# A 192-byte and a 128-byte padding that move where the tiles of a three-layer fp32 kernel begin in SBUF

## Chip, cores and metric

The kernel runs on one core of one Trainium2 chip. The time is the device time of one execution in microseconds; of several executions the median counts. Profiles are of one execution, taken by the hardware profiler. SBUF is the on-chip memory of 128 partitions from which all engines read; a tile's address is a byte offset that is the same in each partition.

## What is computed

Two blocks act on a sequence of 512 tokens with 1,024 features, all in fp32. The first has two layers, the second one. Cut to what costs time:

```python
# first block, layer 0: gated 3-tap convolution beside 8-head attention with low-rank q, k, v and rope
x = x + rms_norm(parallel_conv_mla(rms_norm(x, g0), ...), g1)
x = x + rms_norm(square(relu(rms_norm(x, g2) @ w1)) @ w2, g3)      # w1 1024x4096, w2 4096x1024
# layer 1: 31-tap depthwise convolution between two pointwise products, layer norm, silu
x = x + rms_norm(conformer_conv(rms_norm(x, g4), ...), g5)
x = x + rms_norm(square(relu(rms_norm(x, g6) @ w1)) @ w2, g7)
# second block, one layer: 16 meta tokens in front, forgetting attention (8 heads), pooling, swiglu
h = h + concat(attention, pooled) @ w_out
h = h + (silu(n2 @ w_gate) * (n2 @ w_up)) @ w_down                 # 1024x2816 twice, 2816x1024
```

Nearly all of it is matrix products of weights with all 512 tokens.

## The kernel before, in words

Activations lie with features on partitions and tokens along the row. Every fp32 operand of a product is split into two fp32r parts, a rounded one (plane 0, "hi") and the rest (plane 1, "lo"), and every product is made of three TensorE matmuls (`mm3`, lines 357 to 359): hi weights by hi tokens, hi weights by lo tokens, lo weights by hi tokens. A matmul has a stationary operand of 128 columns, loaded first by LDWEIGHTS (the profile's PEld), and a moving operand of up to 512 columns that streams past it.

The tiles come from pools, and where a pool's tiles lie follows from the order in which the pools and the constants are laid out, with nothing that chooses an address:

- pool `c`, the constants: `vec` (all small vectors in one table), `eps`, `ones`, `onesf`, `ident`, `bd` and others, made in `consts` and `late_consts`
- pool `p`, 32 token tiles named `P` of 4,096 bytes in each partition: the split activations (two planes of 512), pairs of unsplit ones, and the split q, k, v and probabilities of both attentions
- pool `s`, nine scratch tiles `S` of 2,176 bytes
- pool `r`, three raw weight tiles `raw` of 4,096 bytes; SP's queue loads 512 KB into one at a time (line 271)
- pool `w`, nine split weight tiles `W` of 4,096 bytes: up to four 128-column pieces, hi plane at the start, lo plane 2,048 bytes on. ScalarE rounds (line 284) and VectorE, or GpSimd in the convolution's stage, subtracts (line 286), four tiles ahead of TensorE

In most matmuls the moving operand is a `P` tile and the stationary one a slice of a `W` tile; the profile writes such a group `ps<-P,W`. In the products that make v with tokens as rows it is the other way round (`ps<-W,P`). In attention's scores (line 623) and in its products with v (again lines 357 to 359) both are `P` tiles, and the profile writes `ps<-P`. The `P` tiles' slices begin at multiples of 256 bytes within the tile in nearly all of these; exceptions are the taps of the convolution (`run_pe`), whose moving operand begins at one of 16 successive 4-byte elements, and masked scores that begin at 96, 224 or 352 elements.

The order of the work is the order in which the program is written (two hand-written orders, `B1` and `B2`, interleave attention with other products); no planner chooses it. In the convolution's stage four of eight channel groups run on TensorE (`run_pe`, 384 matmuls of 256 columns) and four on VectorE (line 1082), some taps at a time between TensorE's products (`tick`); the layer norm behind it (line 1177 on) needs both.

Of the kernel before, what the change touches and what calls it, by code (L numbers as in the profile page):

```python
# [11 lines left out]
F32 = mybir.dt.float32  # L12
# [7 lines left out]
DRAM = bass.MemoryType.DRAM  # L20
# [283 lines left out]
class Program:  # L304
# [171 lines left out]

    def consts(self):
        nc, cp = self.nc, self.cpool
        self.vec = cp.tile([128, self.nv], F32, name="vec")
        nc.sync.dma_start(out=self.vec, in_=self.ap["vec"])  # L480
        self.eps = cp.tile([128, 1], F32, name="eps")
        nc.vector.memset(self.eps, EPS)
        self.halfpi = cp.tile([128, 1], F32, name="halfpi")
        nc.vector.memset(self.halfpi, math.pi / 2)
        self.ones = cp.tile([128, 128], F32R, name="ones")
        nc.vector.memset(self.ones.bitcast(F32), 1.0)
        self.onesf = cp.tile([128, 128], F32, name="onesf")
        nc.vector.memset(self.onesf, 1.0)
# [1230 lines left out]
def build(arrays, stop=None):  # L1719
    nc = bacc.Bacc("TRN2", target_bir_lowering=False, num_devices=1)  # L1720
    ap = {}
    for name, a in arrays.items():
        ap[name] = nc.dram_tensor(f"in_{name}", a.shape, mybir.dt.from_np(a.dtype), kind="ExternalInput").ap()
    ap["out"] = nc.dram_tensor("out_0", (D, T), F32, kind="ExternalOutput").ap()
    with tile.TileContext(nc) as tc:
        with tc.tile_pool(name="c", bufs=1) as cp, tc.tile_pool(name="p", bufs=NP) as pp, \
                tc.tile_pool(name="s", bufs=NS) as sp, tc.tile_pool(name="ps", bufs=8, space=PSUM) as psp, \
                tc.tile_pool(name="d", bufs=1, space=DRAM) as dp, \
                tc.tile_pool(name="r", bufs=3) as rp, tc.tile_pool(name="w", bufs=NW) as wp:
            Program(tc, ap, (cp, pp, sp, psp, dp, rp, wp), stop).run()  # L1730
    return nc

# [6 lines left out]
```

## Time and profile before

| | |
|---|---|
| median of 3 runs | 1793.89 us (1792.48 to 1795.05) |
| the profiled execution's own time | 1788.58 us |
| its span, first to last instruction | 1786.8 us |
| TensorE busy | 1746.1 us, 98% of the span |
| VectorE, ScalarE, GpSimd busy | 61%, 45%, 15% |
| mean granted TensorE clock | 0.996 of full speed |

An engine's busy time is the union of its instructions' durations. A matmul's duration overlaps the next one's, so it says little about the pace; the distance from one matmul's start to the next one's start does.

### The profile page before, as it was taken

Reading aid. Unit: us, or ns where it says so; the run is one execution under the profiler, and the core shown is the slowest. Engines: PE = TensorE matmul, PEld = TensorE weight load, DVE = VectorE, ACT = ScalarE, POOL = GpSimd, SP = SyncE. Lnnn points to the kernel's source line nnn. Section 1 sums busy time; section 2 is a strip of 40 time slices with the busy share of each in tenths; the row PEclk is TensorE's granted clock in tenths of the full one; section 3 lists DMA queues with packets and bytes.
Section 4 is the critical chain, followed back from the end, with each engine's and each line's share of the span. In section 5 each row is a group of like instructions: output and inputs, shape, how many; then the busy total and the mean of one; then the engine's idle time right before and its main releaser. Section 6 shows DMA issues by size and latency. Waiting matters only on the chain.

```text
span 1786.8 us, 23140 instructions
## 1 busy us (share of the span) xinstructions
PE 1746.1 (98%) x8828; PEld 1455.2 (81%) x8828; DVE 1092.6 (61%) x1770; ACT 802.0 (45%) x1461; POOL 272.4 (15%) x339
## 2 busy tenths in 40 slices
PE   9999999999999999999999999989999999999999
PEld 7778888888888878998888888888787888888887
DVE  7988685344444789968544444488896554344442
ACT  6546655333333446576433333357675443232230
POOL 3413330000000365503000000042223200000000
PEclk9999999999999999999999999999999999999999
DMA  5232213222222133512222222222222222222221
GB/s 200 68 101 59 101 60 118 94 95 94 95 94 95 48 106 106 166 59 91 100 95 94 95 95 95 94 95 73 72 73 95 94 95 94 95 94 95 94 95 59
DMA packets 49887, 167.26 MB, mean 94 GB/s; under 512 B 6848, under 2 KB 7296, under 8 KB 49776
## 3 DMA queue, kind: packets, MB, share of 16 engines
q1 hardware_dynamic: 47776, 160.70, 27.0%
q0 software_dynamic: 1936, 5.07, 1.0%
q8 instruction: 69, 1.13, 0.3%
q14 instruction: 42, 0.34, 0.1%
q10 hardware_dynamic: 64, 0.02, 0.0%
HBM read 158.25 MB, written 4.19 MB: 91 GB/s over the span
## 4 chain that ended last, share of the span: by engine, by line
PE 81%; DVE 11%; issue 3%; ACT 2%; POOL 2%; DMA 1%; SPq 0%; POOLq 0%; DVEq 0%; ACTq 0%
PE ps L358 26%; PE ps L357 26%; PE ps L359 26%; DVE P L968 2%; DVE W L286 1%; PE ps L623 1%; DVE P L401 1%; DVE S L424 1%; POOL P L971 1%; ACT S L450 1%; DVE S L1477 1%; DVE P L398 1%; DVE S L422 1%; DMA P<-in_xT 1%; DVE P L636 0%
## 5 line engine op out<-in xcount | busy, mean ns | idle before, releaser
L357 PE MATMUL ps<-P,W 128*128 128x512 f32 (+1 forms) x2541 | 935.2, 368 | 6.9 <-DVE S L1130 3.1
L358 PE MATMUL ps<-P,W 128*128 128x512 f32 (+1 forms) x2541 | 932.1, 367 | 5.8 <-DVE P L401 5.8
L359 PE MATMUL ps<-P,W 128*128 128x512 f32 (+1 forms) x2541 | 930.9, 367 | 0.0
L284 ACT ACTIVATE W<-raw 128x512 fp32r<-128x512 f32 x578 | 356.9, 628 | 672.9 <-PE ps L359 586.3
L286 DVE TENSOR_TENSOR W<-raw,W 128x512 fp32r<-128x512 f32 x523 | 372.2, 719 | 396.8 <-ACT W L284 391.1
L357 PEld LDWEIGHTS ps<-P,W 128*128 128x128 f32 x2541 | 479.9, 189 | 93.2 <-DVE S L1130 3.5
L358 PEld LDWEIGHTS ps<-P,W 128*128 128x128 f32 x2541 | 480.3, 189 | 90.2 <-DVE P L401 7.2
L359 PEld LDWEIGHTS ps<-P,W 128*128 128x128 f32 x2541 | 480.0, 189 | 84.4 <-DVE W L286 0.4
L971 POOL TENSOR_TENSOR P<-P 128x256 f32<-128x256 f32 x48 | 45.5, 957 | 787.9 <-DVE P L968 786.8
L398 DVE TENSOR_TENSOR P<-S,P 128x512 fp32r<-128x512 f32 (+3 forms) x134 | 93.8, 705 | 50.5 <-ACT P L397 49.9
L397 ACT ACTIVATE P<-S 128x512 fp32r<-128x512 f32 (+3 forms) x134 | 81.4, 613 | 63.2 <-DVE S L1664 25.8
L286 POOL TENSOR_TENSOR W<-raw,W 128x512 fp32r<-128x512 f32 x55 | 73.6, 1369 | 38.0 <-ACT W L284 33.9
L1082 DVE SCALAR_TENSOR_TENSOR ps<-P,vec,ps 128x512 f32<-128x512 f32 x116 | 77.8, 745 | 0.0
L1029 DVE SCALAR_TENSOR_TENSOR S<-ps,S 128x512 f32<-128x512 f32 x64 | 43.7, 690 | 37.0 <-PE ps L359 36.7
L400 ACT ACTIVATE P<-P,vec 128x256 fp32r<-128x256 f32 (+1 forms) x80 | 43.7, 550 | 49.8 <-POOL P L971 30.3
L470 POOL TENSOR_TENSOR S<-S 128x256 f32<-128x256 f32 (+1 forms) x45 | 47.6, 1058 | 76.0 <-ACT S L469 73.6
L401 DVE SCALAR_TENSOR_TENSOR P<-P,vec 128x256 fp32r<-128x256 f32 (+1 forms) x80 | 53.2, 678 | 9.7 <-ACT P L400 9.5
L469 ACT ACTIVATE S<-P 128x256 f32<-128x256 f32 (+1 forms) x105 | 46.4, 473 | 17.8 <-DVE P L1056 11.8
L636 POOL TENSOR_TENSOR P<-S,P 128x512 fp32r<-128x512 f32 (+1 forms) x24 | 34.3, 1428 | 113.0 <-DVE P L635 96.1
L1049 DVE TENSOR_TENSOR P<-ps,P 128x512 f32<-128x512 f32 x42 | 29.1, 692 | 30.9 <-PE ps L359 30.9
L623 PE MATMUL ps<-P 128*128 128x512 f32 (+3 forms) x160 | 41.3, 376 | 1.8 <-DVE S L1443 0.8
L470 DVE TENSOR_TENSOR S<-S 128x256 f32<-128x256 f32 (+1 forms) x60 | 33.0, 550 | 14.5 <-ACT S L469 13.5
(262 smaller groups left out, 1295.6 us busy)
## 6 DMA issues: line engine op xcount, KB each, us to landing
raw<-in_w SPq DMA_DIRECT2D x286, 512.0 KB
P<-in_xT SPq DMA_DIRECT2D x8, 256.0 KB
P<-in_xT POOLq DMA_DIRECT2D x8, 256.0 KB, 5.6
keep<-P SPq DMA_DIRECT2D x8, 256.0 KB
P<-P SPq DMA_DIRECT2D x16, 128.0 KB
P<-keep POOLq DMA_DIRECT2D x8, 256.0 KB, 4.6
out<-P SPq DMA_DIRECT2D x7, 256.0 KB
raw<-in_w SPq DMA_DIRECT2D x2, 256.0 KB
```

The costliest lines, as they stand in the source:

```text
L284: nc.scalar.activation(out=w[:, 0, :cols], in_=r, func=AF.Copy)
L286: eng.tensor_sub(out=w[:, 1, :cols], in0=r, in1=w[:, 0, :cols].bitcast(F32))
L357: mm(ps, w[0], x[0], start=first, stop=False)
L358: mm(ps, w[0], x[1], start=False, stop=False)
L359: mm(ps, w[1], x[0], start=False, stop=last)
L397: nc.scalar.activation(out=hi, in_=src, func=AF.Copy)
L398: nc.vector.tensor_sub(out=lo, in0=src, in1=hi.bitcast(F32))
L401: nc.vector.scalar_tensor_tensor(out=lo, in0=src, scalar=scale, in1=hi.bitcast(F32), op0=OP.mult, op1=OP.subtract)
L470: (eng or nc.vector).tensor_add(out=acc, in0=acc, in1=t)
L623: mm(o[:m], k, q[:, pl, c0:], start=n == 0 and m == 128, stop=n == len(keys) - 1 and mask is None)
L971: ins = eng.tensor_add(out=x[k][:, cols], in0=x[k][:, cols], in1=m[k][:, cols]).ins
L1082: V.scalar_tensor_tensor(out=dst if dst is not None and t == taps[-1] else acc, in0=u, scalar=w, in1=acc, op0=OP.mult, op1=OP.add)
```

## The change

`consts` takes one more tile of 48 floats (192 bytes) in front of `vec`, and a new pool with one tile of 32 floats (128 bytes) stands in front of the pools of raw and split weights. Each is written once, in one column, by a memset on VectorE.

```
     def consts(self):
         nc, cp = self.nc, self.cpool
+        g0 = cp.tile([128, 48], F32, name="pad0")
+        nc.vector.memset(g0[:, 0:1], 0.0)
         self.vec = cp.tile([128, self.nv], F32, name="vec")
...
-                tc.tile_pool(name="d", bufs=1, space=DRAM) as dp, \
+                tc.tile_pool(name="d", bufs=1, space=DRAM) as dp, tc.tile_pool(name="pad", bufs=1) as pad, \
                 tc.tile_pool(name="r", bufs=3) as rp, tc.tile_pool(name="w", bufs=NW) as wp:
+
+            nc.vector.memset(pad.tile([128, 32], F32, name="pad")[:, 0:1], 0.0)
             Program(tc, ap, (cp, pp, sp, psp, dp, rp, wp), stop).run()
```

The built programs place the tiles so (bytes in each partition; the remainder is of the division by 256, the same for all tiles of a pool but `S`):

| tiles | first address before | remainder | first address after | remainder |
|---|---|---|---|---|
| `ones`, `onesf`, `ident`, `bd` | 18240 | 64 | 18432 | 0 |
| `P` | 28736 | 64 | 28928 | 0 |
| `S` | 159808 | 64 and 192 | 160000 | 0 and 128 |
| `raw` | 179392 | 192 | 179712 | 0 |
| `W` | 191680 | 192 | 192000 | 0 |

On all engines the two programs are the same, instruction by instruction, but for the two memsets at the start of VectorE's stream. The piece of the difference on VectorE, at the program's start (`pad` is the new pool's tile, `pad_80` the one in front of the constants; line numbers grow by the added lines):

```order
-L1725 UNCONDITIONAL_BRANCH
-L482 MEMSET eps 128x1
-L484 MEMSET halfpi 128x1
-L486 MEMSET ones 128x128
-L488 MEMSET onesf 128x128
+L1727 UNCONDITIONAL_BRANCH
+L1733 MEMSET pad 128x1
+L480 MEMSET pad_80 128x1
+L484 MEMSET eps 128x1
+L486 MEMSET halfpi 128x1
+L488 MEMSET ones 128x128
+L490 MEMSET onesf 128x128
```

The four memsets that were there move back by two places; nothing else moves.

## Rows read from the trace of the kernel before

**Rows 1.** The page: span, and busy time of each engine.

```profile
span 1786.8 us, 23140 instructions
...
PE 1746.1 (98%) x8828; PEld 1455.2 (81%) x8828; DVE 1092.6 (61%) x1770; ACT 802.0 (45%) x1461; POOL 272.4 (15%) x339
```

**Rows 2.** Matmul groups of line 357, forms kept apart (tiles, shape, count, busy, mean, idle).

```profile
L357 PE MATMUL ps<-P,W 128*128 128x512 f32 x1879 | 743.4, 396 | 5.0 <-DVE S L1130 3.1 <-ACT P L400 1.0 <-ACT W L284 0.9
...
L357 PE MATMUL ps<-P,W 128*128 128x256 f32 x654 | 188.6, 289 | 1.9 <-ACT P L397 0.8 <-ACT P L400 0.6 <-DVE P L1689 0.5
...
L357 PE MATMUL ps<-W,P 128*128 128x256 f32 x80 | 22.9, 286 | 0.0
```

**Rows 3.** Timeline of TensorE in the first MLP (start, duration, instruction).

```profile
449.67 0.40 PE L357 MATMUL ps<-P,W 128*128 128x512 f32 x1
...
455.94 0.40 PE L357 MATMUL ps<-P,W 128*128 128x512 f32 x1
```

**Rows 4.** Timeline of TensorE at the end of the first attention.

```profile
185.53 4.28 PE L623 MATMUL ps<-P 128*128 128x512 f32 x18
189.65 0.39 PE L359 MATMUL ps<-P 128*128 128x512 f32 x1
...
190.56 0.39 PE L357 MATMUL ps<-P 128*128 128x512 f32 x1
...
198.72 0.40 PE L357 MATMUL ps<-P,W 128*128 128x512 f32 x1
```

**Rows 5.** Busy time of engines in two stretches, with clock, DMA share, GB/s.

```profile
190.56:198.72 8.16, 8.16 (x37) 6.76 (x36) 7.21 (x9) 5.40 (x11) 3.28 (x2) 1.00 0.01 3
449.67:455.94 6.27, 6.27 (x29) 5.08 (x27) 3.29 (x5) 2.55 (x5) 0.00 (x0) 1.00 0.33 120
```

**Rows 6.** Timeline of TensorE in products over half the tokens.

```profile
255.48 0.28 PE L357 MATMUL ps<-P,W 128*128 128x256 f32 x1
...
257.97 0.28 PE L357 MATMUL ps<-P,W 128*128 128x256 f32 x1
```

**Rows 7.** Timeline of TensorE in the second attention's maxima.

```profile
1263.23 0.26 PE L1474 MATMUL ps<-P 128*128 128x32 f32 x1
1263.35 0.19 PE L1475 MATMUL ps<-negq,identb 128*128 128x32 bf16 x1
```

**Rows 8.** Matmul groups of line 357 between 645 and 750 us.

```profile
L357 PE MATMUL ps<-P,W 128*128 128x256 f32 x128 | 36.0, 282 | 0.0
...
L357 PE MATMUL ps<-P,W 128*128 128x512 f32 x80 | 31.7, 396 | 3.1 <-DVE S L1130 3.1
```

**Rows 9.** Busy PE, PEld, DVE, ACT, POOL: attention, convolution, second attention.

```profile
62.00:240.00 178.00, 176.25 (x860) 145.71 (x861) 143.83 (x227) 100.69 (x183) 55.37 (x74) 1.00 0.25 81
645.00:750.00 105.00, 102.63 (x628) 91.62 (x629) 104.87 (x159) 54.53 (x93) 60.62 (x61) 1.00 0.38 123
1210.00:1370.00 160.00, 150.63 (x1014) 122.35 (x1014) 137.60 (x276) 106.95 (x225) 37.91 (x45) 0.99 0.23 69
```

**Rows 10.** Timeline of VectorE at the convolution's last taps.

```profile
747.26 1.40 DVE L1082 SCALAR_TENSOR_TENSOR P<-P,vec,ps 128x512 f32<-128x512 f32 x2
```

**Rows 11.** Timeline of TensorE at the layer norm's first sums.

```profile
749.28 2.97 PE L1177 MATMUL ps<-P,onesf 128*128 128x256 f32 x13
```

**Rows 12.** Timeline of the first microseconds, all engines.

```profile
0.89 0.06 DVE L482 MEMSET eps<- 128x1 f32 x1 [0.89 <-PEq L1720]
...
1.20 4.13 PE L722 MATMUL ps<-ones 128*128 128x512 f32 x11 [1.20 <-DVE ones L486]
...
6.25 0.50 PE L357 MATMUL ps<-P,W 128*128 128x512 f32 x1 [0.92 <-ACT W L284]
```

**Rows 13.** The chain that ended last, a piece near the start.

```profile
2.19 4.80 DMA P<-in_xT
```

**Rows 14.** Timeline of TensorE in the first attention, right after `W` products.

```profile
161.93 0.40 PE L357 MATMUL ps<-P 128*128 128x512 f32 x1
...
162.63 0.39 PE L357 MATMUL ps<-P 128*128 128x512 f32 x1
```

## The prediction

> **What bounds the kernel now.** The page comes first: TensorE is busy for 1746.1 of 1786.8 us, the next engine, VectorE, for 61% [rows 1]. So whatever changes TensorE's pace changes the time, and what it waits for is little. The groups by form say what it does with its time: line 357 makes 1,879 matmuls of 512 columns with a `W` tile as weights, and lines 358 and 359 as many, 5,637 in all; 654 times three of 256 columns with `W` as weights, and 80 times three with `W` as the moving operand, 2,202 in all [rows 2]. Their mean durations overlap and give no pace, so I go to the timeline and divide the distance of two starts by the number of matmuls between them.
>
> In the first MLP, 27 steps take 455.94 - 449.67 = 6.27 us, 232.2 ns each [rows 3]. At the end of the first attention the same lines and line 623 run with a `P` tile as weights and a `P` tile as moving operand, with the same 512 columns: 36 steps take 198.72 - 190.56 = 8.16 us, 226.7 ns each [rows 4]. (The stretch counts 37 matmuls with the one already running; the first stretch 29, with the one running and the one that just begins [rows 5].) The clock isn't the reason: both stretches have 1.00 of the full 2.4 GHz. Nor is the other engines' traffic: in the quicker stretch VectorE is busy for 7.21 of 8.16 us, in the slower for 3.29 of 6.27; transfers run in the slower one (0.33 against 0.01), but the same stages keep their pace between loads. What differs is which tiles meet. In all of the slower ones one operand begins 64 bytes past a multiple of 256 and the other 192; in the quicker ones both begin at 64. And `P` tiles lie all over the first 160 KB, so it is not that the two are near each other.
>
> **The change part by part.** (a) *The two memsets.* VectorE's small memset takes 0.06 us [rows 12], so `ones` and the warm-up matmuls that wait for it start up to 0.12 us later. The warm-up ends at 1.20 + 4.13 = 5.33, and the first real matmul starts at 6.25 because it waits for ScalarE's first `W`, which waits for weights [rows 12]: 0.92 us of cover, price nothing; without it 0.12 us.
>
> (b) *The engines' other operands.* `raw` and `W` move together, and so do `P`, `S` and the constants. ScalarE, VectorE and GpSimd never read one of each kind in an instruction, so no pair of theirs changes its relation; only TensorE reads across. Price nothing.
>
> (c) *TensorE, 512 columns.* `P` and `W` now both begin at remainder 0. I take it that what counts is the distance of the two operands modulo 256 bytes: 128 before, 0 after, as for the quicker pairs. Bounds: 0, if it is something else about `W` tiles, and 232.2 - 226.7 = 5.5 ns for each of 5,637 matmuls, 31.0 us. I take the upper end, since the same lines of code make both paces and only the tiles differ.
>
> (d) *TensorE, 256 columns.* 21 steps take 257.97 - 255.48 = 2.49 us, 118.6 ns each [rows 6]. Half of 226.7 would be 113.3, a gain of 5.3. But a matmul of 32 columns with 128 columns of weights holds the next one off for 0.12 us, 0.11 to 0.13 by the rounded starts [rows 7], so the weight load may itself be the floor here and the gain nothing. Between 0 and 5.3 I take 4, nearer to the upper end, since the rows at 512 columns have the same kind of load and are 5.5 apart. Of the 2,202, 3 x 128 = 384 are taps [rows 8], whose moving operand begins at another 4-byte element every three matmuls: distance 0 only now and then, gain 0 (at most 5.3 ns each, 2.0 us). The other 1,818 give 7.3 us, between 0 and 9.6.
>
> (e) *Settling.* Behind `W` products the quick pace comes only after some nine matmuls: the first 18 of that stretch take 189.65 - 185.53 = 4.12 us, 0.04 more than at 226.7 [rows 4]. With some 40 fresh starts, behind waits and behind other kinds of matmul, that is 1.5 us.
>
> (f) *Where TensorE can't use it.* In the convolution VectorE is busy for 104.87 of 105 us [rows 9], its last tap ends at 747.26 + 1.40 = 748.66 [rows 10], and TensorE comes to the sums that need it at 749.28 [rows 11]. So a quicker TensorE will wait there: the 3 x 80 matmuls of 512 columns [rows 8] at 5.5 ns, 1.3 us, are lost. In the two attentions VectorE is busy for 143.83 of 178 and 137.60 of 160 us [rows 9], and chains of VectorE and ScalarE end some of TensorE's waits; these 338 us are 19% of the span, of (c) and (d) 7.2 us, and I give back half, 3.6. Of the first 62 us, where transfers and VectorE lead, half of 1.3.
>
> Sum: 31.0 + 7.3 - 1.5 - 1.3 - 3.6 - 0.6 = 31.3 us. The profiled execution would go from 1788.6 (its span from 1786.8) to 1757; it was 5.3 us under the median of 1793.9, and I take the same difference from that: **1762.5 us**, 1.7% faster. With every loss at nothing and the upper bounds it is 31.0 + 9.6 + 2.0 = 42.6 us; two timeline stamps rounded to 10 ns add 0.4 ns a step, 2 us: 1749.
>
> **A rule that speaks against it.** The Trainium skill, "TensorE: Matmul & The Clock Gate", section "Step-by-step: what each phase is for", says that TensorE reads SBUF through two independent ports, one for the moving operand and one for the weights, and that loading the next weights takes no bandwidth from the running matmul. By that, where the two lie to each other would not matter, and (c) and (d) would be 0. The trace has 226.7 against 232.2 ns for the same work, which that rule does not explain.
>
> **The rivals.** *Nothing changes.* What slows `W` matmuls is something that the paddings leave as it is: their place far up in SBUF (all nine lie above 191 KB, where no quick pair is seen), or that they are written while others are read. Then only the transfers differ: the first token tiles take 4.80 us to land [rows 13], and 6% of two such, 0.6 us, is the most that I see to gain: 1793.3 to 1793.9. For it: no row shows a `W` tile at the quick pace. Against it: TensorE's pace in `W` stretches is the same while VectorE is idle or busy, and `P` tiles between 28 and 160 KB all mix freely. The skill's "DMA: Bandwidth & Descriptors", section "How a descriptor splits into AXI transactions", names blocks of 256 bytes at whose boundaries a transfer is cut, so 4,096 bytes at remainder 192 would touch 17 instead of 16; an estimate by it is that 6%. No row here shows an aligned one.
>
> *Slower: the same remainder collides.* If two streams at the same remainder meet in the same part of SBUF, and the quick pace is a state that only long undisturbed stretches reach, `W` matmuls may stay in what precedes it: 162.63 - 161.93 = 0.70 us for three, 233.3 ns [rows 14], 1.1 ns above 232.2, 6 us over 5,637; with 235, as the rounding allows, 16 us: 1800 to 1810. It decides as soon as the mean stays above 232.2. Against it: the one long stretch settles after nine and stays so.
>
> *Half of it.* Only part of the matmuls settles, because each `W` slice is used for only two or three of them, or the waits in attention take more back than half: 8 to 20 us, 1774 to 1786.
>
> **How the numbers follow.** All or most of the gain 0.72 (1745 to 1774), half of it 0.08, nothing 0.14, slower 0.06. Within 0.2% of 1793.9, some 3.6 us, is about what a measurement tells from no change; the gain and half of it lie below that, so faster 0.80, same 0.14, slower 0.06. The range 1745 to 1788 takes in the first two and leaves out 0.20.
>
> **What would show it.** Right: in the first MLP starts 226 to 227 ns apart, not 230 to 241; 256-column products of lines 357 to 359 at 113 to 116; a wait of TensorE of 1 to 3 us in front of line 1177; VectorE's and ScalarE's durations as before. Wrong: `W` stretches still at 232.2 (then it is the tiles' place or kind), or a quicker pace in the MLPs with new waits of more than 10 us in all elsewhere.

## The result, and the profile after

The changed kernel takes 1761.67 us (median of 4 runs, 1758.98 to 1763.81) against 1794.07 us (4 runs, 1792.48 to 1795.05) in the same comparison: ratio 0.9819, 95% interval 0.9802 to 0.9836, so 1.8% less time, 32.4 us. The forecast was 1762.5 us. The profiled execution took 1762.84 us. Ratios are of executions in the usual state: one of the kernel with the front padding alone, 1906.75 us at a granted clock of 0.847, is left out of its ratio.

The profile of the kernel after has the same instructions and two memsets more; what has shrunk is TensorE's busy time, by 22 us [rows 1]. The operands' work on ScalarE and VectorE has the durations of before (ScalarE's rounding 628 ns both times):

```profile
span 1761.1 us, 23142 instructions
...
PE 1724.0 (98%) x8828; PEld 1460.4 (83%) x8828; DVE 1091.2 (62%) x1772; ACT 801.6 (46%) x1461; POOL 274.0 (16%) x339
...
L284 ACT ACTIVATE W<-raw 128x512 fp32r<-128x512 f32 x578 | 356.6, 628 | 649.9 <-PE ps L359 608.5
L286 DVE TENSOR_TENSOR W<-raw,W 128x512 fp32r<-128x512 f32 x523 | 371.0, 717 | 378.7 <-ACT W L284 376.1
```

The matmul groups of line 357, forms kept apart, answer to [rows 2]. The matmul of 512 columns lasts 392 ns on average instead of 396, which again says little, since durations overlap; that of 256 columns lasts 290 instead of 289:

```profile
L357 PE MATMUL ps<-P,W 128*128 128x512 f32 x1879 | 736.2, 392 | 3.6 <-DVE S L1132 2.8 <-ACT W L284 0.7
...
L357 PE MATMUL ps<-P,W 128*128 128x256 f32 x654 | 189.4, 290 | 1.3 <-ACT P L397 0.8 <-DVE P L1691 0.5
```

The starts say what happened. TensorE's timeline after, first in the products over half the tokens (it answers to [rows 6]; columns are start, duration, instruction), then in the first MLP (to [rows 3]):

```profile
253.33 0.28 PE L357 MATMUL ps<-P,W 128*128 128x256 f32 x1
...
255.84 0.28 PE L357 MATMUL ps<-P,W 128*128 128x256 f32 x1
...
443.12 0.39 PE L357 MATMUL ps<-P,W 128*128 128x512 f32 x1
...
449.24 0.39 PE L357 MATMUL ps<-P,W 128*128 128x512 f32 x1
```

From 443.12 to 449.24 there are 27 steps again: 6.12 us, 226.7 ns each, where it was 232.2. From 253.33 to 255.84 there are 21: 2.51 us, 119.5 ns each, where it was 118.6. So the quick pace has come to these products of 512 columns and not to these of 256; over the whole trace 96% of the 512-column steps with `W` are at 228 ns or less, where it was 8%.

Windows of the kernel after (busy PE, PEld, DVE, ACT, POOL, granted clock, DMA share, GB/s), in order: the first attention, the first MLP, the convolution from its first 512-column product to the layer norm's first sum, the second MLP, the second attention:

```profile
62.00:238.00 176.00, 175.08 (x866) 146.00 (x865) 143.69 (x226) 100.35 (x183) 55.33 (x74) 1.00 0.26 81
276.00:590.30 314.30, 314.30 (x1447) 262.81 (x1446) 142.07 (x213) 116.92 (x196) 0.63 (x1) 1.00 0.29 94
637.13:738.60 101.47, 101.47 (x624) 91.56 (x625) 101.44 (x155) 53.93 (x90) 59.22 (x61) 0.98 0.38 122
838.90:1156.40 317.50, 317.50 (x1462) 265.51 (x1461) 147.61 (x234) 119.48 (x202) 1.60 (x2) 1.00 0.29 95
1191.95:1354.75 162.80, 153.42 (x1013) 124.94 (x1013) 137.67 (x276) 107.10 (x226) 38.10 (x45) 0.97 0.24 72
```

In both MLPs TensorE is busy from end to end at the full clock. Measured from the same instruction to the same instruction in the two traces, the first went from 321.9 to 314.5 us and the second from 325.0 to 317.5, 15.0 us together; the swiglu of the second block, again with 512 columns, gave 10.3 more. The convolution went from 102.7 to 102.3. The second attention took 2.6 us more, at a granted clock of 0.97 where [rows 9] had 0.99.

At the convolution's end the cover that [rows 10, 11] showed is gone, and no wait has come in its place. The last taps on VectorE, and TensorE's first sums of the layer norm:

```profile
737.24 1.40 DVE L1084 SCALAR_TENSOR_TENSOR P<-P,vec,ps 128x512 f32<-128x512 f32 x2
...
738.60 3.62 PE L1179 MATMUL ps<-P,onesf 128*128 128x256 f32 x16
```

The taps end at 738.64 and the sums begin at 738.60; before, TensorE came 0.62 us after the last tap. At the start the added memsets push the warm-up matmuls from 1.20 to 1.25. In this execution they then last 5.06 us instead of 4.13, and the first product starts at 7.05 instead of 6.25 [rows 12]. The memsets are not the reason: the kernel with distance 96 (below) has them too and starts it at 6.25. The timeline after, then that kernel's:

```profile
0.92 0.06 DVE L480 MEMSET pad<- 128x1 f32 x1
...
1.25 5.06 PE L724 MATMUL ps<-ones 128*128 128x512 f32 x11 [1.25 <-DVE ones L488]
...
7.05 0.80 PE L357 MATMUL ps<-P,W 128*128 128x512 f32 x1 [0.74 <-ACT W L284]
```

```profile
6.25 0.63 PE L357 MATMUL ps<-P,W 128*128 128x512 f32 x1
```

The traces of this pair differ by 25.7 us only, less than the medians. I come back to that below.

### The profile page after: what moved, and what is told of

It reads as the page before. It is cut to its first block, busy times and chain, and to the rows that moved or that the text cites. A ratio compares the mean times of both kernels' runs of the same rounds, so it can differ in the third digit from the quotient of the medians.

```text
span 1761.1 us, 23142 instructions
## 1 busy us (share of the span) xinstructions
PE 1724.0 (98%) x8828; PEld 1460.4 (83%) x8828; DVE 1091.2 (62%) x1772; ACT 801.6 (46%) x1461; POOL 274.0 (16%) x339
## 4 chain that ended last, share of the span: by engine, by line
PE 81%; DVE 11%; issue 3%; ACT 2%; POOL 2%; DMA 1%; SPq 0%; POOLq 0%; ACTq 0%; DVEq 0%
PE ps L357 26%; PE ps L358 26%; PE ps L359 26%; DVE P L970 1%; PE ps L625 1%; DVE W L286 1%; POOL P L973 1%; DVE P L401 1%; DVE S L1479 1%; DVE S L424 1%; DVE P L398 1%; DVE S L422 1%; DMA raw<-in_w 1%; ACT S L450 0%; DVE S L420 0%
## 5 line engine op out<-in xcount | busy, mean ns | idle before, releaser
L401 DVE SCALAR_TENSOR_TENSOR P<-P,vec 128x256 fp32r<-128x256 f32 (+1 forms) x80 | 54.3, 692 | 10.9 <-ACT P L400 10.7
```

What stands on the lines that cost most here:

```text
L401: nc.vector.scalar_tensor_tensor(out=lo, in0=src, scalar=scale, in1=hi.bitcast(F32), op0=OP.mult, op1=OP.subtract)
```

## The experiments

**Theory** (theory 1 below). What counts is the distance of the stationary from the moving operand's first byte, modulo 256: 128 before, 0 after. **Rivals.** It is where `W` lies in itself (its own remainder, theory 3, or a place far up in SBUF that the change moved a little); or both kinds must begin at a multiple of 256 (theory 2 prices each kind by itself); or the transfers gain, since `raw` begins at a multiple too. In all but the last three experiments the remainders of `P`, `raw` and `W` are set by the size of the paddings alone. For each the pace is given as the mean distance of starts over all steps of a kind, the convolution's taps apart; steps that are over 16 ns off, waits and spells at half clock (1.2 instead of 2.4 GHz), are left out.

**Half of the change: the front padding alone.** `P` at 0, `raw` and `W` at 128.

```
-            nc.vector.memset(pad.tile([128, 32], F32, name="pad")[:, 0:1], 0.0)
```

> Only the padding in front of the constants: P at remainder 0, raw and W at 128, so their distance is 128 as before. Theory 1 (the distance of the two operands modulo 256 counts): as before, ratio 0.998 to 1.002, 512-column starts 232 ns apart. Theory 2 (each operand has its own price off a multiple of 256; P is the moving one in nearly all matmuls): at least half of the gain, ratio 0.99 or less, about 229 ns or less. Theory 3 (W's own remainder counts alone, 0 is good): as before.

Measured: 1794.81 us, ratio 1.0002 (0.9989 to 1.0016), 232.7 ns for 512 columns. `P` and the constants at a multiple of 256 are worth nothing by themselves.

**The other half: the padding in front of the weights alone.** `P`, `raw` and `W` all at 64.

```
-        g0 = cp.tile([128, 48], F32, name="pad0")
-        nc.vector.memset(g0[:, 0:1], 0.0)
```

> Only the padding in front of the weights: P at remainder 64, raw and W at 64, distance 0, nothing on a multiple of 256. Theory 1: the whole gain, ratio 0.980 to 0.984, starts 226.7 ns apart. Theories 2 and 3: as before, ratio near 1, 232 ns, since no operand is on a multiple of 256.

Measured: 1761.73 us, ratio 0.9823 (0.9798 to 0.9847), the whole gain, with no tile of the two kinds at a multiple of 256. In the first MLP of this kernel 27 steps take 6.12 us, 226.7 ns, and of the one with the front padding alone 6.27 us, 232.2 ns; the timelines of TensorE, the one with the weights' padding first:

```profile
446.25 0.39 PE L357 MATMUL ps<-P,W 128*128 128x512 f32 x1
...
452.37 0.39 PE L357 MATMUL ps<-P,W 128*128 128x512 f32 x1
```

```profile
449.90 0.40 PE L357 MATMUL ps<-P,W 128*128 128x512 f32 x1
...
456.17 0.40 PE L357 MATMUL ps<-P,W 128*128 128x512 f32 x1
```

So that both kinds begin at a multiple of 256 isn't what counts; their distance is. The place of `W` up in SBUF isn't it either: here it moves up by 128 bytes and keeps a remainder of 64.

**Other distances.** `P` stays at 0, and the size of `pad` moves `raw` and `W` together. First 64 and 192:

```
-            nc.vector.memset(pad.tile([128, 32], F32, name="pad")[:, 0:1], 0.0)
+            nc.vector.memset(pad.tile([128, 48], F32, name="pad")[:, 0:1], 0.0)
```

(and `[128, 16]` for 192)

> Both paddings, the second 64 bytes longer: P at 0, W at 64, distance 64. Theory 1 says only that 0 is good and 128 is not; if the streams meet in four parts of 64 bytes, 64 is a case of its own: between 227 and 236 ns, ratio 0.98 to 1.01. Theory 3: as before, 232 ns. Which value it has tells whether only distance 0 is good.

> Both paddings, the second 64 bytes shorter: P at 0, W at 192 as before the change, distance 192. Theory 1: not the whole gain, 228 to 236 ns, ratio 0.985 to 1.01. Theory 2: half of the gain, since P is on a multiple of 256. Theory 3: as before, since W's remainder is that of before.

Measured: at 64 1792.11 us, ratio 0.9992 (0.998 to 1.0004); at 192 1772.65 us, ratio 0.9883 (0.9862 to 0.9904). That `W` at remainder 64 is quick when `P` is at 64 and slow when `P` is at 0 takes away the rival that `W`'s own remainder decides. The timeline of TensorE with distance 64, first over half the tokens, then in the first MLP:

```profile
255.71 0.28 PE L357 MATMUL ps<-P,W 128*128 128x256 f32 x1
...
258.10 0.28 PE L357 MATMUL ps<-P,W 128*128 128x256 f32 x1
...
450.56 0.39 PE L357 MATMUL ps<-P,W 128*128 128x512 f32 x1
...
456.86 0.39 PE L357 MATMUL ps<-P,W 128*128 128x512 f32 x1
```

The two kinds of products part here: 27 steps of 512 columns take 6.30 us, 233.3 ns, the slowest so far, and 21 steps of 256 columns 2.39 us, 113.8 ns, the quickest so far. So the load of the weights is not a floor at 119 ns. With distance 192 the MLP's 27 steps take 6.18 us, 228.9 ns:

```profile
446.80 0.39 PE L357 MATMUL ps<-P,W 128*128 128x512 f32 x1
...
452.98 0.39 PE L357 MATMUL ps<-P,W 128*128 128x512 f32 x1
```

Then the distances between, with `[128, 40]`, `[128, 56]`, `[128, 8]` and `[128, 24]` floats for distances of 32, 96, 160 and 224 bytes.

> P at 0, W at 32. Measured so far for the pace with 512 and 256 columns: distance 0: 226.9 and 119.8 ns, 64: 233.3 and 115.0, 128: 232.6 and 119.0, 192: 229.1 and 117.4. If the distance acts smoothly, 32 lies between 0 and 64: about 230 and 117, ratio 0.990. If it acts by whole blocks of 64 bytes, 32 is as 0 or as 64: ratio 0.982 or 0.999.

> P at 0, W at 96. Smoothly: between 64 and 128, about 233 and 117 ns, ratio 1.000. By blocks: as 64 (233.3 and 115.0) or as 128 (232.6 and 119.0). Slower than before by over 0.2% only if the worst place lies here.

> P at 0, W at 160. Smoothly: between 128 and 192, about 231 and 118 ns, ratio 0.994. By blocks: as 128 (1.000) or as 192 (0.988).

> P at 0, W at 224. Smoothly: between 192 and 0, about 228 and 118.6 ns, ratio 0.985. By blocks of 64: as 192 (0.988) or as 0 (0.982). If the best place of the 512-column products lies a little under 0, at or under 226.9 ns.

The pace in ns of each distance of `W` from `P`, 256 columns apart by which operand is the moving one (`P` in `ps<-P,W`, `W` in `ps<-W,P`), and the ratio to the kernel before:

| distance | 512, `P` moves | 256, `P` moves | 256, `W` moves | ratio (95%) |
|---|---|---|---|---|
| 0 (the change) | 226.9 | 119.8 | 119.5 | 0.9819 (0.9802 to 0.9836) |
| 32 | 233.3 | 118.3 | 116.9 | 1.0013 (1.0000 to 1.0025) |
| 64 | 233.3 | 115.0 | 117.7 | 0.9992 (0.9980 to 1.0004) |
| 96 | 234.2 | 118.5 | 119.7 | 1.0038 (1.0027 to 1.0048) |
| 128 (before) | 232.5 | 119.1 | 118.7 | 1 |
| 160 | 233.3 | 119.8 | 118.2 | 1.0018 (1.0005 to 1.0031) |
| 192 | 229.1 | 117.4 | 115.8 | 0.9883 (0.9862 to 0.9904) |
| 224 | 233.3 | 117.0 | 118.3 | 1.0018 (1.0003 to 1.0034) |

For 512 columns 0 is best, 192 gives about two thirds of the gain in time, and the pace of everything else lies within 2 ns. The smooth reading fails: at 32 and 224 it had 230 and 228 ns, and both measure 233.3; a reading by whole blocks of 64 bytes fits 32, 96 and 160 to about 1 ns, but not 224, which is slower than both its neighbours. With `W` moving, the distance of the stationary from the moving operand is the negative of the first column. Read so, the two columns for 256 agree row by row within 0.8 ns (32 with `P` moving and 224 with `W` moving both have 118.3, 64 and 192 have 115.0 and 115.8): what counts is the signed distance of stationary from moving, whichever tile is which. Only 96 is slower than before by more than 0.2%: 6.8 us by the ratio, and by the pace 5,637 times 1.7 ns, 9.6 us, less the 256-column products' share. At 160 and 224 the ratio is 1.0018, and the intervals begin just above 1. Its timeline in the first MLP, 6.33 us for 27 steps:

```profile
451.76 0.40 PE L357 MATMUL ps<-P,W 128*128 128x512 f32 x1
...
458.09 0.39 PE L357 MATMUL ps<-P,W 128*128 128x512 f32 x1
```

**The raw weights' part.** `raw` at 192 as before the change, `P` and `W` at 0: `pad` of 16 floats in front of `raw`, and another of 16 between `raw` and `W`.

```
-                tc.tile_pool(name="r", bufs=3) as rp, tc.tile_pool(name="w", bufs=NW) as wp:
+                tc.tile_pool(name="r", bufs=3) as rp, tc.tile_pool(name="pad1", bufs=1) as pad1, \
+                tc.tile_pool(name="w", bufs=NW) as wp:
...
-            nc.vector.memset(pad.tile([128, 32], F32, name="pad")[:, 0:1], 0.0)
+            nc.vector.memset(pad.tile([128, 16], F32, name="pad")[:, 0:1], 0.0)
+            nc.vector.memset(pad1.tile([128, 16], F32, name="pad1")[:, 0:1], 0.0)
```

> P and W at 0 as after the change, the raw tiles alone back at remainder 192 (64 bytes of padding in front of them, 64 between them and W). If transfers, ScalarE's rounding or VectorE's subtraction had a part in the gain, some of it goes: 0.6 us or more, and more where those engines lead. Theory 1: nothing goes, ratio 0.982, 226.9 ns at 512 columns.

Measured: 1766.13 us, ratio 0.9835 (0.9821 to 0.985), paces 226.9, 119.8 and 119.5 ns as with the whole change. The interval overlaps that of the change (0.9802 to 0.9836). Most of the gain is there without `raw`; that its place is worth some microseconds is neither shown nor excluded.

**Each kind at its best distance.** Can 256 columns have 64 while 512 keep 0? The `W` tile must then be longer than 4,096 bytes; a control has eight tiles of 4,352 bytes instead of nine, and takes seven blocks ahead instead of eight at two places. The second kernel puts a block that is used mostly by 256-column products 16 floats in (1,488 matmuls); the third also puts the blocks of v 48 floats in.

```
-NP, NS, NW = 32, 9, 9
+NP, NS, NW = 32, 9, 8
...
-            w = self.w_pool.tile([128, 2, T], F32R, name="W")
+            o = 16 if self.half(self.nsplit) else 0
+            w = self.w_pool.tile([128, 1088], F32R, name="W")[:, o:o + 1024].rearrange("p (a b) -> p a b", a=2)
...
-            self.W.more(8)
+            self.W.more(7)
```

(in the control `half` is always false; in the third, 48 for `v` and `vv`)

> The control of the next two: after the change, with eight W tiles of 4,352 bytes instead of nine of 4,096, each still at remainder 0, and the early weight blocks at the stage boundaries taken seven ahead instead of eight. Expected as after the change, ratio 0.980 to 0.985; if the ninth tile was needed, some us slower.

> As the control, but weight blocks that only 256-column products use begin 64 bytes into their W tile: 1,488 matmuls over half the tokens at distance 64, the 512-column ones still at 0. If the number of columns decides which distance is good: those matmuls go from 119.8 to 115.0 ns, 7 us less in TensorE's stream, ratio 0.003 to 0.004 below the control where the waits of the boundaries don't take it back. If the distance acts by the tile and not by the columns, the 512-column pace suffers, or nothing is won.

> As the one before, and the weight blocks of v, which are the moving operand there, begin 192 bytes into their tile, so that the stationary P lies 64 past them: 228 more 256-column matmuls go from 119.5 to about 116 ns, 0.8 us less. That is at the edge of what the times tell; the starts show it.

| | time, us | ratio (95%) | 512 | 256, `P` moves | 256, `W` moves |
|---|---|---|---|---|---|
| control, eight tiles | 1779.75 | 0.9915 (0.9901 to 0.9929) | 226.9 | 119.8 | 119.5 |
| 256-column blocks at 64 | 1776.66 | 0.9898 (0.9881 to 0.9915) | 226.9 | 115.1 | 119.5 |
| and v's at 192 | 1775.77 | 0.9893 (0.9878 to 0.9908) | 226.9 | 115.3 | 116.0 |

The pace did what the table of distances says: it changed for the blocks that were moved and stayed for the others. TensorE's timeline over half the tokens, 30 steps, in the control (3.60 us, 120.0 ns each), then with the blocks moved (3.40 us, 113.3 ns each):

```profile
238.46 0.28 PE L374 MATMUL ps<-P,W 128*128 128x256 f32 x1
...
242.06 0.28 PE L374 MATMUL ps<-P,W 128*128 128x256 f32 x1
```

```profile
236.50 0.28 PE L374 MATMUL ps<-P,W 128*128 128x256 f32 x1
...
239.90 0.28 PE L374 MATMUL ps<-P,W 128*128 128x256 f32 x1
```

But 1,488 matmuls at 4.7 ns are 7.0 us, and 3.1 came out between control and second, 4.0 between control and third, with intervals that overlap. Of the ten executions of the two, eight are under the control's quickest (1777.56 us), so some gain in time is likely; that it is the whole 7.0 is not shown.

And the control, for which 0.980 to 0.985 was expected, has 0.9915: with eight tiles it is 17 us slower by the ratios than the change with its nine, and 13.6 us slower than the kernel with `raw` apart, which was run beside it. That is more than there is to win. The waits of TensorE that the trace names sum to 40.0 us against 32.9 in the kernel after. The rest can lie in the clock: the control's five executions are at 0.984 to 0.987 of full speed, the four with `raw` apart at 0.990 to 0.993. Its profiled one:

```profile
core 0: 1779.7 us, clock 0.985
```

By (1 - 0.985) x 1779.7 = 26.7 us, against 15.8 in the kernel after (below), the half clock can have cost up to 10.9 us more. No run tells whether the tiles' number, their length or the seven blocks ahead brought it. No version beat the change.

## Why the forecast was right, step by step

**What bounds the kernel** held: TensorE is still busy for 98%, and a change of its pace alone moved the end.

**(c), 512 columns, the distance modulo 256**, was right in cause and size. By step, 5,584 pairs of the same matmul in the two traces give 31.3 us (232.5 to 226.9 ns); forecast 31.0. The two halves of the change show the cause: the tiles at 64 bytes past a multiple gain as much as those on it, and `P` alone on it gains nothing. The sum of 31.3 has (e) in it: 4% of the steps after are still above 228 ns. The step that carried the forecast was to let one row of `P` by `P` [rows 4] stand for what `W` would do at the same distance. The rule of the Trainium skill that was weighed there ("TensorE: Matmul & The Clock Gate", section "Step-by-step: what each phase is for": two independent ports, a load that takes no bandwidth) isn't borne out by these runs: with the same instructions, the relation of two addresses moves the pace from 226.9 to 234.2 ns.

**(a) and (b)**, the memsets and the other engines, priced at nothing, show no cost: the first product's start isn't set by the memsets, and ScalarE's rounding keeps its 628 ns.

**(d), 256 columns**, failed: 7.3 us forecast, 0.7 lost (119.06 to 119.76 with `P` moving, 118.7 to 119.5 with `W` moving, 1.3 us together; the 384 taps, forecast at nothing, won 0.5, from 119.3 to 117.9). That it would follow the 512-column rows was wrong, and so was the floor by the weights' load that I set beside it: 113.8 ns is reached in products that have the same load. It prefers another distance, 64 (192 with `W` moving, which is 64 the other way round).

**(e) and (f), settling and stages that can't use the pace**, 7.0 us in all, need the times to be told apart. In the profiled pair the first 62 us gained 0.55 (forecast 0.65) and the first attention 1.6 (forecast half of 3.8, 1.9). In the convolution 0.4 was left, and the second attention lost 2.6 instead of gaining 1.7. Both of these come with the clock of this one execution: after the change a spell at half clock, with starts 427 ns apart, falls into the convolution, and 10.2 us of half clock into the second attention, where before has 3.4. Kernels with the same pace whose spells fall as before's tell more. The convolution's window in the kernel before and in the one with `raw` apart, then the second attention's in the kernel before and in the one with the weights' padding alone:

```profile
647.37:749.28 101.91, 101.91 (x624) 90.97 (x625) 101.89 (x156) 53.86 (x90) 58.25 (x60) 1.00 0.38 123
641.30:741.12 99.82, 99.82 (x625) 90.44 (x626) 99.80 (x152) 53.60 (x90) 59.45 (x61) 1.00 0.37 122
1210.05:1370.22 160.17, 150.81 (x1014) 122.47 (x1014) 137.56 (x276) 107.09 (x226) 38.09 (x45) 0.99 0.23 69
1196.34:1356.45 160.11, 150.54 (x1013) 122.49 (x1013) 136.88 (x274) 106.95 (x226) 36.53 (x42) 0.99 0.23 68
```

In the convolution the pace is worth 2.1 us then. Part of it is lost again, but inside the layer norm's sums and not in front of them: with `raw` apart the last tap ends at 742.84, 1.72 us after the first sum starts, and the 16 sums take 4.21 us instead of the 3.62 of the kernel after:

```profile
741.12 4.21 PE L1179 MATMUL ps<-P,onesf 128*128 128x256 f32 x16
741.43 1.41 DVE L1084 SCALAR_TENSOR_TENSOR P<-P,vec,ps 128x512 f32<-128x512 f32 x2
```

So (f) took the first sums to need the last tap, which they don't, and gave back 1.3 us where some 0.6 is lost. In the second attention it was too hopeful the other way: at an equal clock nothing is gained, where 1.7 was forecast. Over all stages, waits and steps at half clock grew by 5.6 us in the profiled pair, which with 31.3 - 0.7 leaves 25.0 of the 25.7 that the traces differ by; the rest is in the other kinds of matmul.

**The step from the profiled execution to the median.** The forecast for the profiled execution, 1757 us, was wrong: it took 1762.84. I took the 5.3 us between before's profiled execution and its median as lasting; after, the profiled execution is 1.2 us above the median. The forecast of the median was not hurt by it, since it is the same as the median before less 31.3 us. The view of spans and granted clocks, a line from each kernel (before, the front padding alone, after):

```profile
core 0: 1786.8 us, clock 0.996
```

```profile
core 0: 1794.1 us, clock 0.994
```

```profile
core 0: 1761.1 us, clock 0.991
```

The kernel with the front padding alone has before's median (1794.81), and its profiled span is 7.3 us longer than before's. Against that span the kernel after is 33.0 us shorter, as the medians say. So before's profiled execution was a quick one. One part of it can be the clock: (1 - 0.996) x 1786.8 = 7.1 us and (1 - 0.991) x 1761.1 = 15.8 us are the most that the half clock can have cost in the two, 8.7 us apart. The 58 executions of the kernel before that stand beside the experiments differ among themselves as much: clocks from 0.989 to 0.997, times from 1788.47 to 1799.41 us.

So 1762.5 against 1761.67 is partly luck: the 7.3 us of (d) that didn't come and the 7.0 of (e) and (f), of which the medians leave little to see (32.4 us of gain, by the interval 29 to 36, against 30.6 of TensorE's stream), cancel. The main term, (c), was not luck.

**The rivals.** *Nothing changes* fell with the first MLP's 226.7 ns. *Slower, the same remainder collides* fell with it; of eight distances only 96 makes the kernel slower by more than 0.2%, and equal remainders are the best. *Half of it* did not happen, since 96% of the 512-column steps with `W` are at the quick pace. Of the signs, the 256-column products at 113 to 116 ns and the wait in front of line 1177 did not show.

## What to carry to other kernels

This was seen with fp32r products that load a stationary operand for each matmul; no run here has another type. Where matmuls follow each other without a wait, divide the distance of two starts by the steps between, for each pair of tiles that meet; two paces for the same shape are the sign to look at the addresses of both operands. Then look at the difference of their addresses modulo 256 and not at each one's alignment, and try its multiples of 64 with a padding, for each number of columns by itself. A padding must not cost a buffer: the kernel with one `W` tile less was some 17 us slower, more than the 7 us that the better distance could have brought.

## What the runs showed of the hardware

The best paces are 226.7 ns for 512 columns and 113.3 ns for 256, 544 and 272 cycles at 2.4 GHz, 17/16 of the columns. 512 columns have the best at distance 0 and 256 columns at 64, and at the four distances tried that aren't multiples of 64, 512 columns lie at 233.3 to 234.2 ns. Why it is 0 for the one and 64 for the other, and why 192 gives two thirds, stays open; so does whether `raw`'s place counts. That the pace repeats every 256 bytes is not shown in full either: the distances of `W` from `P` that were tried all lie from 128 below to 96 above one value, 192000 - 28928 = 163072 = 637 x 256.

In the profiled pair the quicker kernel shows a lower mean clock (0.991 against 0.996). Its rows put 0.98 in the convolution, where VectorE is busy for 101.44 of 101.47 us, and 0.97 in the second attention, where TensorE has gaps (153.42 of 162.80 us busy); the MLPs are at 1.00. But its four executions have 0.991 to 0.994, and those of the kernel before 0.989 to 0.997, so it is not shown that the pace lowers the clock. The kernels with eight `W` tiles are at 0.984 to 0.987 in all 15 executions; why is open.
